# A second up-projection group planned as four tile pairs by seven products instead of three, with a different set of tiles whose low parts come by adding transfers

## The chip, the core and the metric

The kernel runs on one core of a Trainium2 chip. Its time is the device time of one execution in microseconds (us); a time given for a kernel is the median of several executions. Engines are called as in the profile: PE (matrix products), PEld (its weight loads), DVE (vector), ACT (scalar), POOL (GpSimd), SP (sync, which only issues transfers). Matrix products write PSUM banks; everything else lies in SBUF.

## What is computed

One decoder layer on 512 tokens with 1024 channels: a convolution branch and a gated linear attention branch, merged, and then a channel mixer. The change lies in the channel mixer alone:

```python
u2 = _rmsnorm(h, norm2_g[l])
z = _causal_dwconv(u2 @ w_ffn_up[l], ffn_dw_w[l], ffn_dw_b[l])
h = h + (jax.nn.silu(z[..., :FFN_DIM]) * z[..., FFN_DIM:]) @ w_ffn_down[l]
```

`w_ffn_up` has 1024 rows and 2 x 2816 columns. In tiles of 128 columns that is 22 tiles of the first half (a, 0 to 21) and 22 of the second (b, 22 to 43); channel tile i of the mixer needs a-tile i and b-tile 22 + i. The depthwise convolution has three taps in time.

## The kernel before, in words

**Products in two parts.** Every float32 operand is split into a high part (rounded by a cast on ACT) and a low part (the rest), and a product is the sum of three: low by high, high by low, high by high (`mm3`, L538 to L544). For a weight tile, `split_weight` (L415 on) writes the high part on ACT (L427 or L457). The low part is made in one of two ways for a tile of its own: DVE subtracts (L465), or, if the tile is in the set `ADDED`, ACT writes the negative of the rounded tile (L459) and a transfer on POOL's queue adds the original from memory to it (L460). For the tiles of `ADDED` in the up projection `late_low_tile` (L563) runs all products by the high part first and the eight by the low part last.

**Plain channel tiles.** Tiles i and 22 + i are each multiplied with all 512 tokens: 8 row blocks x 3 = 24 products of 512 columns a tile, 48 a channel tile.

**Channel tiles by seven products.** `two_tiles` (L1353 on) treats tile i, tile 22 + i, the two halves of the rows and the two halves of the tokens as 2 x 2 blocks, and takes seven block products instead of eight: 7 x 4 row blocks x 3 = 84 products of 256 columns. Its weight operands come in four parts: x1 (two block products, tile i itself), x3 (two, a sum of blocks of both tiles), x2 (two), x4 (one, half as wide). POOL adds the blocks: three additions of 128x512 behind the split of x1, a fourth behind that of x3 (L399). Four block products write bank x one after the other; after three of them ACT copies an interim result out of x or y (L1360), or DVE subtracts or adds it (L1363), before the next block product may go on in the same bank. The results lie in two `tmp` tiles, c1 and c2; there are six `tmp` buffers, and each channel tile's convolution takes two more (L1739 on ACT, L1742 on DVE).

**Order.** The up projection runs in four groups' worth of channel tiles: first 0 and 2 as a start, then the lists in `PLANS`, each followed by a part of the down projection (`seven`, L1513 adds its results to `hres`). A list has entries by kind; `up_plan` turns each into a sequence of steps of PE: a part of a seven-product unit, a piece of a plain tile (row blocks a to b), or a role. A role ("first" or "second" in a pair of channel tiles) is the tail of a channel tile: convolution taps, SiLU, gating (L1756), differences and sums for the down projection (L1772, L1782 to L1784) and their splits (L1761 on ACT, L1762 on DVE). Behind the last product of a unit nothing on PE waits for its role until the down projection; a unit's x1 is moved ahead of roles that stand directly before it. In the kind `both` two units share one plain tile pair: x1, x3, a1, x2, a2, x4 of the first, then the second's x1, x3, b1, x2, b2, x4. In the kinds `opens`, "" and `closes` one unit goes with one plain channel tile, and a piece of it stands between any two successive parts of the unit (`opens` begins with a piece, too).

**Looking ahead.** `weight` splits two operands ahead of the one in use, `refill` issues loads (on SP, L309 and L305) two ahead of that; there are four raw tiles, four for high and four for low parts. A planner puts the instructions of each engine in one fixed order, by the order of the program and by its own estimates of when each can run.

Of the kernel before, what the change touches and what calls it, by code (L numbers as in the profile page):

```python
# [28 lines left out]
FT = FF // P  # L29
# [3 lines left out]
O_PAIRS = ((0, 2), (1, 3), (4, 6), (5, 7))  # L33
GROUPS = (((0, 2), (1, 3), (4, 6), (5, 7)), ((8, 10), (9, 11), (20, 21)), ((12, 14), (13, 15), (16, 18), (17, 19)))
PLANS = (
(("plain",1,3),("both",4,6,5),("closes",7,8)),(("opens",10,9),("",11,20),("closes",21,12)),(("opens",14,13),("",15,16),("",18,17),("plain",19)),)
AHEAD = 6

MERGE = [("w_gb", 6, 7), ("w_ga", 0, 1), ("w_ga", 2, 3), ("w_ga", 4, 5), ("w_ga", 6, 7)]
# [9 lines left out]
ADDED = {("w_glu", j) for j in range(4, 2 * KT)} | {("w_qk", m) for m in range(KT)}  # L49
ADDED |= {("w_v", KT // 2 + j) for j in range(KT // 2)} | {("w_gb", m) for m in range(AHEAD)}  # L50
POOLED = {("w_qk", 0), ("w_qk", 1)}
ADDED -= POOLED
ADDED |= {("w_up", j) for j in (1, 23, 3, 25, 8, 9, 31, 20, 35, 16, 39, 19, 41)}
RATE = 5.0
ROWS = (0, 5, 5, 5, 8, 8, 8, 8)
EVERY = (6, 6, 6, 6, 4, 4, 4, 4)
# [47 lines left out]
def trunk_layer(ctx: ExitStack, tc: tile.TileContext, a: dict, out: bass.AP):  # L104
# [28 lines left out]
    def heap(dt=F32):  # L133
        return hp.tile([P, T], dt, tag="h", name=nm("h"))
# [57 lines left out]
    def up_plan(gi):  # L192

        pairs = GROUPS[gi]
        whole = range(KT)

        def parts(q):
            return [("part", q, part) for part in ("x1", "x3", "x2", "x4")]

        def cut(m, *at):  # L200
            return [("tile", m, range(a, b)) for a, b in zip((0, *at), (*at, KT))]

        def turns(m, role):
            return [("tile", m, whole), ("tile", FT + m, whole), (role, m)]

        def one(q, f, kind):

            x1, x3, x2, x4 = parts(q)
            if kind == "opens":
                (a1, a2), (b1, b2, b3) = cut(f, 4), cut(FT + f, 4, 6)  # L210
                seq = [a1, x1, a2, x3, b1, x2, b2, x4, role(q), b3]
            elif kind == "closes":
                a1, a2, a3 = cut(f, 3, 6)
                seq = [x1, a1, x3, a2, x2, a3, x4, role(q), ("tile", FT + f, whole)]
            else:
                (a1, a2), (b1, b2) = cut(f, 5), cut(FT + f, 4)
                seq = [x1, a1, x3, a2, x2, b1, x4, role(q), b2]
            return seq + [role(f)]

        def both(p, q, f):  # L220

            x1, x3, x2, x4 = parts(p)
            y1, y3, y2, y4 = parts(q)
            (a1, a2), (b1, b2) = cut(f, 4), cut(FT + f, 4)
            return [*(x1, x3, a1, x2, a2, x4, y1, y3, role(p), b1, y2, b2, y4, role(q)), role(f)]

        seconds = {q for _, q in pairs}

        def role(i):
            return ("second" if i in seconds else "first", i)  # L230

        plan = []
        for kind, *units in PLANS[gi]:
            if kind == "plain":
                for i in units:
                    plan += turns(i, role(i)[0])
            elif kind == "both":
                plan += both(*units)
            else:
                plan += one(*units, kind)  # L240
        for n in range(1, len(plan)):
            at = n
            while plan[n][0] == "part" and plan[n][2] == "x1" and at and plan[at - 1][0] in ("first", "second"):
                plan[at - 1], plan[at] = plan[at], plan[at - 1]
                at -= 1
        return plan
# [32 lines left out]
    for gi, pairs in enumerate(GROUPS):  # L279
        if gi == 0:  # L280
            order += [("w_up", j) for i in pairs[0] for j in (i, FT + i)]
            first = len(order) + 6
        else:
            first = len(order)
        order += up_order(up_plan(gi))
        tight |= set(range(first, len(order)))
        order += [("w_down", (pairs, step, d)) for step, d in STEPS]
# [1370 lines left out]
    for p, q in O_PAIRS:  # L1658

        f1 = merged(p)  # L1660
        both = heap(F32R)
# [203 lines left out]
    banks, values, units = {}, {}, {}  # L1865
    third, found_parts = [], {}
    for gi, pairs in enumerate(GROUPS):
        acts = []
        if gi == 0:
# [8 lines left out]
            p, q = pairs[0]  # L1878
# [13 lines left out]
        else:  # L1892
            found = first_of_pair(w)
        for what, i, *rest in up_plan(gi):
            if what == "tile":
                if 0 in rest[0]:
# [130 lines left out]
```

## Time and profile before

| | |
|---|---|
| median of 3 runs | 819.51 us (819.47 to 819.72) |
| the profiled execution, its own time | 820.0 us |
| its span, first to last instruction | 818.3 us |
| PE busy | 807.3 us, 99% |
| DVE, ACT, POOL busy | 691.1 (84%), 501.8 (61%), 212.1 (26%) us |
| transfers | 120.43 MB, mean 147 GB/s |
| mean granted clock of PE | 0.997 |

A row of the timeline gives the start and the duration in us, the engine, the line, the operation, what it writes and reads, and in brackets how long the engine was idle before and what ended that. A product's shown duration is longer than the distance to the next one, since products are pipelined: the pace is read from the starts. The channel mixer takes PE from about 487 us on; the list of the second group (`PLANS[1]`) starts at 605.92 us, and its part of the down projection at about 669 us.

### The profile page before, as it was taken

How to read it: one execution, taken by the hardware profiler on the slowest of the kernel's cores; microseconds unless marked ns; L12 is line 12 of the kernel's file. 1: busy time of each engine (PE TensorE's matmuls, PEld its weight loads, DVE VectorE, ACT ScalarE, POOL GpSimd, SP SyncE). 2: the span in 40 equal slices, each digit the busy share in tenths (PEclk: the TensorE clock that was granted, in tenths of full speed). 3: DMA queues.
4: the chain of work that ended last, by engine and by line, in shares of the span. 5: the costliest groups of instructions: out<-in, count | busy, mean ns of one | idle time of the engine just before them, and what ended most of it. 6: DMA issues, size and time to landing. Idle time of an engine off the chain costs nothing.

```text
span 818.3 us, 11590 instructions
## 1 busy us (share of the span) xinstructions
PE 807.3 (99%) x4263; PEld 695.1 (85%) x4263; DVE 691.1 (84%) x1091; ACT 501.8 (61%) x763; POOL 212.1 (26%) x193
## 2 busy tenths in 40 slices
PE   9999999999999999999999999999999999999996
PEld 7888888888888899989888898898889987899885
DVE  6779999998998878486778888989956999688895
ACT  6667788677547565493534656567355664467544
POOL 2025433332203332122001113340133311532012
PEclk9999999999999999999999999999999999999998
DMA  8488858645831232422448544256655346446762
GB/s 334 147 196 178 187 161 189 147 123 135 182 105 48 80 127 78 153 105 88 170 131 209 177 121 112 78 180 181 130 159 175 129 107 163 129 129 209 203 129 103
DMA packets 38346, 120.43 MB, mean 147 GB/s; under 512 B 3897, under 2 KB 9153, under 8 KB 38289
## 3 DMA queue, kind: packets, MB, share of 16 engines
q1 hardware_dynamic: 28912, 86.39, 29.4%
q0 software_dynamic: 9360, 33.30, 22.8%
q8 instruction: 33, 0.54, 0.3%
q14 instruction: 25, 0.20, 0.1%
q10 hardware_dynamic: 16, 0.00, 0.0%
HBM read 117.58 MB, written 2.10 MB: 146 GB/s over the span
## 4 chain that ended last, share of the span: by engine, by line
PE 76%; DVE 18%; issue 2%; DMA 2%; ACT 1%; POOL 0%; POOLq 0%; SPq 0%; DVEq 0%; ACTq 0%
PE mm L542 15%; PE mm L543 15%; PE mm L544 15%; PE mm L563 7%; DVE c L911 5%; PE cv L542 3%; PE cv L543 3%; PE cv L544 3%; DVE aside L911 3%; DVE tmp L1742 2%; PE ax L543 2%; PE ax L544 2%; PE mm L765 2%; PE ax L542 2%; DVE wlo L428 2%
## 5 line engine op out<-in xcount | busy, mean ns | idle before, releaser
L542 PE MATMUL mm<-uh,wlo 128*128 128x512 f32 (+1 forms) x444 | 161.3, 363 | 0.0
L543 PE MATMUL mm<-ul,whi 128*128 128x512 f32 (+1 forms) x444 | 158.9, 358 | 0.0
L544 PE MATMUL mm<-uh,whi 128*128 128x512 f32 (+1 forms) x444 | 158.9, 358 | 0.0
L428 DVE TENSOR_TENSOR wlo<-raw,whi 128x1024 fp32r<-128x1024 f32 x86 | 105.0, 1227 | 36.7 <-ACT whi L427 35.2
L399 POOL TENSOR_TENSOR raw<-raw,raw 128x512 f32<-128x512 f32 x42 | 66.7, 1589 | 187.4 <-DVE wlo L428 116.1
L427 ACT CAST whi<-raw 128x1024 fp32r<-128x1024 f32 x86 | 82.6, 966 | 39.7 <-PE mm L544 26.8
L542 PEld LDWEIGHTS mm<-uh,wlo 128*128 128x128 f32 x444 | 83.9, 189 | 12.6 <-DVE wlo L465 0.3
L544 PEld LDWEIGHTS mm<-uh,whi 128*128 128x128 f32 x444 | 83.8, 189 | 12.4
L543 PEld LDWEIGHTS mm<-ul,whi 128*128 128x128 f32 x444 | 83.9, 189 | 12.0
L457 ACT CAST whi<-raw 128x1024 fp32r<-128x1024 f32 x78 | 81.3, 1046 | 20.7 <-PE mm L544 14.1
L459 ACT ACTIVATE wlo<-raw 128x1024 fp32r<-128x1024 f32 x41 | 43.2, 1059 | 34.2 <-PE mm L542 19.0
L427 ACT CAST whi<-kept 128x1024 fp32r<-128x1024 f32 (+1 forms) x40 | 40.3, 1009 | 33.7 <-DVE kept L375 16.9
L428 DVE TENSOR_TENSOR wlo<-kept,whi 128x1024 fp32r<-128x1024 f32 (+1 forms) x40 | 47.7, 1193 | 11.5 <-ACT whi L427 11.5
L911 DVE SCALAR_TENSOR_TENSOR c<-aside,btmp,c 128x247 f32<-128x247 f32 (+13 forms) x93 | 51.8, 562 | 0.0
L911 DVE SCALAR_TENSOR_TENSOR aside<-cv,pp,aside 128x255 f32<-128x255 f32 (+6 forms) x112 | 51.8, 462 | 0.0
L465 DVE TENSOR_TENSOR wlo<-raw,whi 128x1024 fp32r<-128x1024 f32 x35 | 45.2, 1299 | 5.6 <-ACT whi L457 5.4
L911 DVE SCALAR_TENSOR_TENSOR c<-cv,pp,c 128x247 f32<-128x247 f32 (+13 forms) x93 | 43.0, 463 | 1.4 <-ACT c L907 1.4
L1742 DVE SCALAR_TENSOR_TENSOR tmp<-mm,pp,tmp 128x511 f32<-128x511 f32 (+1 forms) x46 | 34.1, 742 | 4.3 <-ACT tmp L1739 4.1
L563 PE MATMUL mm<-ul,whi 128*128 128x512 f32 x88 | 34.4, 391 | 0.0
L563 PE MATMUL mm<-uh,whi 128*128 128x512 f32 x88 | 34.3, 390 | 0.0
L1742 DVE SCALAR_TENSOR_TENSOR tmp<-tmp,pp,tmp 128x511 f32<-128x511 f32 (+1 forms) x36 | 31.0, 878 | 1.5 <-ACT tmp L1739 1.2
L1360 ACT COPY tmp<-mm 128x256 f32<-128x256 f32 x32 | 11.8, 369 | 26.9 <-PE mm L544 25.7
(519 smaller groups left out, 2220.2 us busy)
## 6 DMA issues: line engine op xcount, KB each, us to landing
raw<-in_w_up_dram SPq DMA_DIRECT2D x44, 512.0 KB, 4.8
raw<-in_w_glu_dram SPq DMA_DIRECT2D x16, 512.0 KB, 5.3
raw<-in_w_down_dram SPq DMA_DIRECT2D x15, 512.0 KB, 5.9
wlo<-in_w_up_dram POOLq DMA_DIRECT2D x13, 512.0 KB, 6.9
wlo<-in_w_glu_dram POOLq DMA_DIRECT2D x12, 512.0 KB, 6.9
kept<-in_w_down_dram POOLq DMA_DIRECT2D x10, 512.0 KB, 5.7
raw<-in_w_v_dram SPq DMA_DIRECT2D x8, 512.0 KB, 6.7
raw<-in_w_qk_dram SPq DMA_DIRECT2D x8, 512.0 KB, 6.0
```

The source lines that it names most:

```text
L399: work = nc.gpsimd.tensor_tensor(out, x, y, ALU.add)
L427: nc.scalar.copy(hi, raw)
L428: two_low[:] = [nc.vector.tensor_tensor(lo, raw, hi.bitcast(F32), ALU.subtract)]
L457: nc.scalar.copy(hi, raw)
L459: pace[0] = nc.scalar.mul(lo, raw, -1.0)
L465: pace[0] = nc.vector.tensor_tensor(lo, raw, hi.bitcast(F32), ALU.subtract)
L542: nc.tensor.matmul(acc, ll, rh, start=first, stop=False, **kw)
L543: nc.tensor.matmul(acc, lh, rl, start=False, stop=False, **kw)
L544: nc.tensor.matmul(acc, lh, rh, start=False, stop=last, **kw)
L563: nc.tensor.matmul(acc, x[:, k * P : (k + 1) * P], acts[k][n], start=at == 0, stop=at == len(parts) - 1)
L911: nc.vector.scalar_tensor_tensor(out[:, j:], x[:, : half_t - j], w, out[:, j:], ALU.mult, ALU.add)
L1742: nc.vector.scalar_tensor_tensor(z[:, s:], acc[:, : T - s], w[j], z[:, s:], ALU.mult, ALU.add)
```

## The change

`PLANS[1]` gets two entries in place of three. Before, units by seven products are 10, 11 and 21, and 9, 20 and 12 are plain; after, units are 10, 9, 20 and 21, and 11 and 12 are plain. A new kind, `both_close`, orders 20, 21 and 12. The order of the roles stays 10, 9, 11, 20, 21, 12. `ADDED` loses 9, 31 and 20, and gains 5, 27, 30, 11, 33, 12 and 34, so 18 tiles of the up projection are in it where 13 were. Of the tiles that are plain in both kernels, 5, 27, 30, 12 and 34 change from DVE's subtraction to the adding transfer.

```diff
 PLANS = (
-(("plain",1,3),("both",4,6,5),("closes",7,8)),(("opens",10,9),("",11,20),("closes",21,12)),(("opens",14,13),("",15,16),("",18,17),("plain",19)),)
+(("plain",1,3),("both",4,6,5),("closes",7,8)),(("both",10,9,11),("both_close",20,21,12)),(("opens",14,13),("",15,16),("",18,17),("plain",19)),)
-ADDED |= {("w_up", j) for j in (1, 23, 3, 25, 8, 9, 31, 20, 35, 16, 39, 19, 41)}
+ADDED |= {("w_up", j) for j in (1, 23, 3, 25, 5, 27, 8, 30, 11, 33, 12, 34, 13, 35, 16, 39, 19, 41)}
+        def both_close(p, q, f):
+            x1, x3, x2, x4 = parts(p)
+            y1, y3, y2, y4 = parts(q)
+            a1, a2, a3, a4 = cut(f, 2, 4, 6)
+            return [x1, a1, x3, x2, x4, y1, a2, y3, role(p), a3, y2, a4, y4, role(q), ("tile", FT + f, whole), role(f)]
...
-            elif kind == "both":
-                plan += both(*units)
+            elif kind.startswith("both"):
+                plan += {"both": both, "both_close": both_close}[kind](*units)
```

## The prediction, made before the changed kernel ran

> **What bounds the kernel now.** I read the page first, then the list of who waited for whom on PE, the chain of waits, and the stretches of the channel mixer.
>
> ```profile
> span 818.3 us, 11590 instructions
> ...
> PE 807.3 (99%) x4263; PEld 695.1 (85%) x4263; DVE 691.1 (84%) x1091; ACT 501.8 (61%) x763; POOL 212.1 (26%) x193
> ```
>
> ```profile
> PE mm L542 <- DVE hres L1513: 0.6, 1, 0.6
> PE mm L542 <- ACT tmp L1360: 0.4, 1, 0.4
> ```
>
> ```profile
> 551.00:569.00 18.00, 18.00 (x109) 16.01 (x108) 18.00 (x28) 11.89 (x18) 1.80 (x3) 1.00 0.61 183
> 606.00:622.00 16.00, 16.00 (x103) 14.55 (x102) 8.40 (x9) 6.93 (x11) 6.95 (x6) 1.00 0.49 143
> 622.00:645.00 23.00, 23.00 (x151) 21.01 (x150) 19.36 (x27) 14.87 (x21) 7.47 (x6) 1.00 0.39 115
> 645.00:660.00 15.00, 15.00 (x101) 13.76 (x100) 14.17 (x20) 9.54 (x15) 1.74 (x1) 1.00 0.48 169
> ```
>
> PE is the bound: busy without a hole in all four stretches (columns: length, then busy us of PE, PEld, DVE, ACT, POOL; clock, transfer share). So time is won only by fewer columns on PE or by ending one of its short waits, and is lost wherever a new wait begins. DVE is full in two places, 551 to 569 and 645 to 660, where the roles of channel tiles pile up, so there it covers little more.
>
> **The change part by part: products.** One channel tile goes from 48 products of 512 columns to 84 of 256.
>
> ```profile
> 761.74 10.88 PE mm L563 x48
> ```
>
> ```profile
> 608.64 0.28 PE L542 MATMUL cv<-uh,wlo 128*128 128x256 f32 x1
> ...
> 611.51 0.40 PE L563 MATMUL mm<-uh,whi 128*128 128x512 f32 x1
> ```
>
> The chain holds 48 wide products in 10.88 us, 0.2267 each. Between the two starts of the timeline lie 24 narrow ones: 2.87 us, 0.1196 each, over half of a wide one. 84 take 10.05, so **0.83 us** goes, wherever the products are issued without a hole. The Trainium skill (TensorE: Matmul & The Clock Gate, Back-to-back issue gap) has N / 2.4 + 2.5 ns: 215.8 and 109.2 ns, which as an estimate would save 1.19 us; both rows here are longer, the narrow one by more, and I keep to them.
>
> **Low parts.** Tiles 5, 27, 30, 12 and 34 lose a subtraction of some 1.14 us on DVE, and get an ACT pass and a POOL issue, as do the new plain tiles.
>
> ```profile
> L459 ACT ACTIVATE wlo<-raw 128x1024 fp32r<-128x1024 f32 x41 | 43.2, 1059 | 34.2 <-PE mm L542 19.0 <-PE ax L542 10.4 <-PE cv L542 3.1
> ...
> L460 POOL DMA_DIRECT2D wlo<-in_w_up_dram x13 | 11.3, 868 | 49.6 <-ACT wlo L459 48.4 <-DMA raw<-in_w_up_dram 1.1
> ...
> wlo<-in_w_up_dram POOLq DMA_DIRECT2D x13, 512.0 KB, 6.9
> ```
>
> Five more passes (5 x 1.06 on ACT, 5 x 0.87 on POOL) and 2.5 MB beside 120 hide behind PE: ACT is busy 61%, POOL 26%. What they relieve is seen at two waits of PE in the first group:
>
> ```profile
> 512.32 1.21 DVE L465 TENSOR_TENSOR wlo<-raw,whi 128x1024 fp32r<-128x1024 f32 x1
> ...
> 516.19 0.74 DVE L1742 SCALAR_TENSOR_TENSOR tmp<-mm,pp,tmp 128x510 f32<-128x510 f32 x1
> ...
> 517.02 0.63 ACT L1750 ACTIVATE tmp<-tmp 128x512 f32<-128x512 f32 x1 [0.27 <-DVE tmp L1742]
> ...
> 517.25 0.28 PE L544 MATMUL ax<-uh,whi 128*128 128x256 f32 x1
> ...
> 517.56 0.35 ACT L1360 COPY tmp<-mm 128x256 f32<-128x256 f32 x1
> ...
> 517.96 0.38 PE L542 MATMUL mm<-xq,wlo 128*128 128x256 f32 x1 [0.43 <-ACT tmp L1360]
> ...
> 518.19 0.28 PE L543 MATMUL mm<-usq,whi 128*128 128x256 f32 x1
> ```
>
> Unit 4 goes from x1 to x3 with no piece between. Its copy out of bank x stands on ACT behind a SiLU that waits for a tap on DVE, and DVE is late by tile 5's subtraction (512.32), among others. PE starts 517.96 for a due 517.37, and loses another 0.11 in restarting: 0.70. Without the 1.14 the copy comes in time: **-0.70** (bounds -0.70 and 0, if ACT's extra pass takes its place).
>
> ```profile
> 557.72 1.23 DVE L465 TENSOR_TENSOR wlo<-raw,whi 128x1024 fp32r<-128x1024 f32 x1
> ...
> 577.34 1.22 DVE L428 TENSOR_TENSOR wlo<-raw,whi 128x1024 fp32r<-128x1024 f32 x1
> ...
> 578.15 0.39 PE L542 MATMUL ax<-whi,al 128*128 128x512 f32 x1
> 578.62 0.50 PE L543 MATMUL ax<-wlo,ah 128*128 128x512 f32 x1
> 578.95 0.40 PE L544 MATMUL ax<-whi,ah 128*128 128x512 f32 x1
> ```
>
> At 578 a low part of the down projection is late at the end of a DVE queue in which tile 30's subtraction stood; the two gaps of 0.47 and 0.33 exceed 0.227 by 0.34 in all: **-0.34** (bounds -0.34 and 0). The price of the transfer: tile 30's low part is due 16 products, 3.6 us, after the tile begins; 1.06 + 0.87 + 6.9 us of pass, issue and landing have to start some 5 us before the tile. Between +1.1 (pass right behind the present cast, 556.63 to 557.69) and 0; I take 0, because ACT has holes of 0.6 and 0.8 us just ahead of that cast.
>
> **The new order, `both_close`.** Unit 20's x3, x2 and x4 follow each other with nothing between, while DVE works off the roles of 9 and 11. The nearest rows are those of unit 7 in the first group: it, too, follows a `both`, whose two roles (6 and 5) fall on it; but pieces of tile 8 stand between its parts.
>
> ```profile
> 546.24 0.28 PE L542 MATMUL mm<-uh,wlo 128*128 128x256 f32 x1
> ...
> 549.85 1.78 DVE L1742 SCALAR_TENSOR_TENSOR tmp<-tmp,pp,tmp 128x511 f32<-128x511 f32 x1
> ...
> 553.81 0.74 DVE L1742 SCALAR_TENSOR_TENSOR tmp<-tmp,pp,tmp 128x510 f32<-128x510 f32 x1
> ...
> 554.66 0.37 ACT L1360 COPY tmp<-mm 128x256 f32<-128x256 f32 x1 [0.64 <-DVE tmp L1742]
> ...
> 559.80 0.41 DVE L1363 TENSOR_TENSOR tmp<-tmp,mm 128x256 f32<-128x256 f32 x1
> ...
> 560.36 0.29 PE L542 MATMUL mm<-uh,wlo 128*128 128x256 f32 x1
> ```
>
> Count from x1's first product, 546.24. The copy that x2 has to wait for cannot start before the role's taps free a `tmp` buffer (553.81), and ends 8.79 us on. In `both_close` x2 is due after x1, a piece of six and x3: 2.87 + 1.36 + 2.87 = 7.10. **+1.74**, with the 0.05 from copy to product seen at 517.91 (bounds 0, if the planner gives c2 a buffer earlier, and 1.74). Behind the waiting x2 stands all of PE.
>
> Then x4 has to wait for a subtraction out of the same bank. Unit 7's ended at 13.97, 0.15 us before its x4 (560.36). `both_close` wants it at 7.10 + 1.74 + 2.87 = 11.71. Bounds 0 and +2.26; I take the row's place less the 1.14 that tile 30's subtraction held in that queue: **+1.1**. What follows gets no further wait in the sum, since each of these gives DVE and POOL time.
>
> The start of the list, `both` directly behind the down projection, costs nothing: DVE is busy 8.4 of 16 us there and ACT 6.9. POOL's four more additions (1.6 us each) fit its 26%. The largest wait left stays:
>
> ```profile
> 683.16 0.87 POOL L389 DMA_DIRECT2D kept<-in_w_down_dram  x1 [0.33 <-issue]
> ...
> 692.25 0.62 ACT L427 CAST whi<-kept 128x512 fp32r<-128x512 f32 x1 [2.18 <-DMA kept<-in_w_down_dram]
> ...
> 693.35 0.39 PE L544 MATMUL mm<-whi,yh 128*128 128x512 f32 x1
> ...
> 694.34 0.47 PE L542 MATMUL mm<-whi,al 128*128 128x512 f32 x1 [0.61 <-DVE hres L1513]
> ```
>
> An adding transfer of the down projection lands 9 us after its issue, and PE loses 0.99 - 0.23 + 0.08 = 0.84. Roles 21 and 12 and the last tile end the list as before, so 0 (bounds -0.84 and 0).
>
> **Sum:** -0.83 - 0.70 - 0.34 + 1.74 + 1.1 = +0.97 us. It is made in the profiled execution (820.0 us, 1.7 outside its span), which stands 0.5 above the median; the difference is carried to the median: 819.51 + 0.97 = **820.5**.
>
> **The rivals.** *The order costs nothing.* The planner knows the list and may put copy and subtraction ahead of role work, as nothing else on PE hangs on that; both waits near 0. Then -1.87: 817.6, or 816.8 with the wait at 694 gone too; with the waits half there 819.1. For it: in the rows it lets short instructions into the holes of chains of taps. Against: in unit 7 the subtraction stood behind ten us of role work though its product was ready 2.3 us earlier.
>
> *DVE's backlog under POOL's additions* (the slower end). Unit 21's blocks can be loaded only when 20's raw tiles come free, so POOL adds them just while DVE works off roles 9 and 11.
>
> ```profile
> 606.03 1.23 DVE L428 TENSOR_TENSOR wlo<-raw,whi 128x1024 fp32r<-128x1024 f32 x1 [1.66 <-ACT whi L427]
> ...
> 617.35 2.66 POOL L399 TENSOR_TENSOR raw<-raw,raw 128x512 f32<-128x512 f32 x2 [6.03 <-DMA raw<-in_w_up_dram]
> ...
> 618.77 2.31 DVE L428 TENSOR_TENSOR wlo<-raw,whi 128x1024 fp32r<-128x1024 f32 x1 [1.97 <-ACT whi L427]
> ```
>
> The same subtraction takes 1.23 alone and 2.31 beside an addition: 1.08 more. With the subtraction for x4 at unit 7's place (2.26) and one or two such delays ahead of it, the waits come to 5.1 to 6.2, the change to +3.2 to +4.3: 822.7 to 823.8. It decides from waits of 3.5 us together on. The Trainium skill (SBUF — State Buffer, Who interferes with whom) says that a vector instruction with two SBUF inputs and a GpSimd one that reads SBUF shut each other out for a whole instruction; the rows agree, and by it four more additions speak against the change.
>
> *The transfers relieve nothing.* DVE's freed time is taken by other late work or the low parts land late; the waits at 517 and 578 stay while the new ones come: -0.83 + 2.84 = +2.0, 821.5.
>
> **How the numbers follow.** About 0.2%, 1.64 us, is what a measurement of this kernel can tell from no change. Forecast 0.40, inside that bound, own range 818.2 to 821.1. Order free 0.26, of which 0.14 is faster by more and 0.12 lies within. Backlog 0.27 and transfers 0.07, both slower by more. So faster 0.14, same 0.52, slower 0.34. The range runs from the free order, 817.4, to the backlog's 823.6.
>
> **What would show it.** Right: no wait at x3 of unit 4 and none at 578's place; PE waiting for L1360 at x2 of unit 20 and for L1363 at its x4; 84 products of 256 columns at 0.12 for unit 9 and unit 20. Wrong: a list of 62 us without a hole on PE (order free), x4 of unit 20 or x1 or x3 of 21 waiting over 3 us, low parts of 30, 33 or 34 as PE's releaser, or a new wait in the third group, whose list is unchanged but planned anew.

## The result, and the profile after

The changed kernel takes 826.24 us (median of 4, 824.67 to 827.43) beside 819.49 for the kernel before (819.04 to 819.72): **+6.75 us, ratio 1.0082 (95% interval 1.0064 to 1.0100)**. The forecast was 820.5, with a range from 817.4 to 823.6. Its profiled execution took 826.04 us. In the ratios below, disturbed executions are left out; this matters for two of the experiments, and one profile could not be used for that reason.

One correction to the text above: the list of tiles in the change leaves out tile 13 (plain, third group), which also gets an adding transfer; with it the 18 are complete. Its cost is tried below.

All lines of the changed file stand 7 further down: L542 is L549, L563 is L570, L1360 is L1367, L1363 is L1370, L428 is L435, L1742 is L1749, L399 is L406; in the experiments some lines stand a few further down again, by their own edits. The page, and the list of who waited for whom on PE (us in total, times, longest):

```profile
span 824.3 us, 11690 instructions
...
PE 809.6 (98%) x4299; PEld 697.8 (85%) x4299; DVE 692.7 (84%) x1091; ACT 509.1 (62%) x774; POOL 221.6 (27%) x202
```

```profile
PE cv L549 <- DVE wlo L435: 2.8, 1, 2.8
PE mm L549 <- ACT tmp L1367: 2.2, 2, 1.5
```

The two waits of before (0.6 behind `hres`, 0.4 at x3 of unit 4) are gone from the list, and longer ones are there. By stage, from the starts on PE:

| stretch | before | after | change |
|---|---|---|---|
| start of the second group's list | 605.92 | 605.70 | -0.22 |
| that list | 63.04 | 69.44 | +6.40 |
| its down projection | 29.58 | 30.30 | +0.72 |
| third group's list | 73.92 | 73.92 | 0 |

So 6.9 us are lost up to the last product; what follows it happens to be 0.9 shorter in this execution (spans 818.3 and 824.3). Nearly all of it lies in the changed list. Rows of the timeline: x3 of unit 4, x4 of unit 7, tile 30 and the down projection in the first group, then the parts of units 20 and 21 in the changed list, and one wait of its down projection:

```profile
517.02 0.39 PE L549 MATMUL mm<-xq,wlo 128*128 128x256 f32 x1
...
559.82 0.39 PE L549 MATMUL mm<-uh,wlo 128*128 128x256 f32 x1 [0.23 <-DVE tmp L1370]
...
564.77 0.39 PE L570 MATMUL mm<-ul,whi 128*128 128x512 f32 x1
565.06 2.11 PE L570 MATMUL mm<-uh,wlo 128*128 128x512 f32 x8
...
578.49 0.50 PE L550 MATMUL ax<-wlo,ah 128*128 128x512 f32 x1 [0.22 <-DVE wlo L435]
...
641.82 0.39 PE L549 MATMUL mm<-xq,wlo 128*128 128x256 f32 x1 [0.63 <-ACT tmp L1367]
...
646.05 0.37 ACT L1367 COPY tmp<-mm 128x256 f32<-128x256 f32 x1 [0.65 <-DVE tmp L1749]
646.48 0.39 PE L549 MATMUL mm<-btmpq,wlo 128*128 128x256 f32 x1 [1.53 <-ACT tmp L1367]
646.59 1.06 ACT L434 CAST whi<-raw 128x1024 fp32r<-128x1024 f32 x1
...
647.37 2.73 POOL L406 TENSOR_TENSOR raw<-raw,raw 128x512 f32<-128x512 f32 x2 [4.89 <-DVE w L1763]
647.78 1.16 DVE L1779 TENSOR_TENSOR w<-w 128x256 f32<-128x256 f32 x1
648.86 1.78 DVE L1763 TENSOR_TENSOR f<-tmp,tmp 128x512 f32<-128x512 f32 x1
649.68 0.40 PE L570 MATMUL mm<-ul,whi 128*128 128x512 f32 x1
650.06 1.71 POOL L406 TENSOR_TENSOR raw<-raw 128x512 f32<-128x512 f32 x1
650.57 2.28 DVE L435 TENSOR_TENSOR wlo<-raw,whi 128x1024 fp32r<-128x1024 f32 x1
652.91 0.39 PE L549 MATMUL cv<-uh,wlo 128*128 128x256 f32 x1 [2.83 <-DVE wlo L435]
...
653.97 0.38 PE L551 MATMUL cv<-uh,whi 128*128 128x256 f32 x1
...
657.50 0.28 PE L549 MATMUL mm<-uh,wlo 128*128 128x256 f32 x1
...
689.01 0.50 PE L550 MATMUL mm<-wlo,sh 128*128 128x512 f32 x1 [0.75 <-DVE wlo L435]
```

Read the changed list from PE's three waits. What PE loses is counted from the time at which the next product was due by the pace, and the "restart" is the extra 0.1 us between the first product after a wait and the second. **x3 of unit 20** (641.82) loses 0.89 with its restart: the copy out of bank x is late on ACT. **x2 of unit 20** (646.48) loses 1.80: its copy could not start before a tap on DVE had freed a buffer. **x1 of unit 21** (652.91) loses 3.10: its low part, whose high part was ready at 647.65, ran only from 650.57 to 652.85, behind two operations of a role. POOL was adding unit 21's blocks (647.37 to 651.77) beside all three operations. They took 1.16, 1.78 and 2.28 us; the same ones take 0.41, 0.68 and 1.21 to 1.23 elsewhere (rows below), 2.9 us less. From 653.97 to 657.50 there are 17 products of 256 columns: 0.21 us each instead of 0.12, 1.5 us lost. The stretches show why:

```profile
650.00:652.90 2.90, 0.08 (x1) 0.00 (x0) 2.90 (x3) 1.56 (x2) 1.77 (x2) 1.00 0.13 51
653.90:657.40 3.50, 3.50 (x19) 3.50 (x19) 3.50 (x7) 1.18 (x2) 0.46 (x1) 0.52 0.00 0
```

Columns: length, busy us of PE, PEld, DVE, ACT, POOL, clock, transfer share, GB/s. About 1 us after PE has restarted from its hole, the granted clock is 0.52 for 3.5 us. Together 0.89 + 1.80 + 3.10 + 1.5 - 0.83 for the saved columns = 6.46, of 6.40 seen.

In the first group, whose list is unchanged, x3 of unit 4 (517.02) lost 0.70 and now loses 0.18. Tile 30's products by the low part begin 0.29 after the one before instead of 0.227. Two things take most of the gain back. x4 of unit 7 (559.82), which did not wait before, now waits for its subtraction and loses 0.43, and 0.1 in restarting. And the wait at 578, which lost 0.34 before, is still there and loses 0.50. So the second list starts only 0.22 earlier, although PE was 0.94 ahead at x3 of unit 4. In the second down projection the wait of 0.84 at 694 is gone, and one that loses 1.15 with its restart stands at 689.01.

### The profile page after: what moved, and what is told of

Its sections match the earlier page's. It is cut to its first block, busy times and chain, and to the rows that moved or that the text cites. A ratio compares the mean times of both kernels' runs of the same rounds, so it can differ in the third digit from the quotient of the medians.

```text
span 824.3 us, 11690 instructions
## 1 busy us (share of the span) xinstructions
PE 809.6 (98%) x4299; PEld 697.8 (85%) x4299; DVE 692.7 (84%) x1091; ACT 509.1 (62%) x774; POOL 221.6 (27%) x202
## 4 chain that ended last, share of the span: by engine, by line
PE 77%; DVE 17%; issue 3%; ACT 2%; DMA 1%; POOL 0%; POOLq 0%; ACTq 0%; DVEq 0%
PE mm L549 15%; PE mm L550 15%; PE mm L551 15%; PE mm L570 6%; DVE c L918 5%; PE cv L549 3%; PE cv L550 3%; PE cv L551 3%; PE cv L570 3%; DVE aside L918 3%; DVE tmp L1749 2%; PE mm L772 2%; PE ax L550 2%; PE ax L551 2%; PE ax L549 2%
## 5 line engine op out<-in xcount | busy, mean ns | idle before, releaser
L549 PE MATMUL mm<-uh,wlo 128*128 128x512 f32 (+1 forms) x412 | 146.5, 356 | 0.2 <-DVE tmp L1370 0.2
L550 PE MATMUL mm<-ul,whi 128*128 128x512 f32 (+1 forms) x412 | 144.0, 350 | 0.0
L551 PE MATMUL mm<-uh,whi 128*128 128x512 f32 (+1 forms) x412 | 144.0, 350 | 0.0
L435 DVE TENSOR_TENSOR wlo<-raw,whi 128x1024 fp32r<-128x1024 f32 x90 | 108.7, 1216 | 34.8 <-ACT whi L434 33.8
L406 POOL TENSOR_TENSOR raw<-raw,raw 128x512 f32<-128x512 f32 x45 | 68.8, 1528 | 189.6 <-DVE wlo L435 109.7
L549 PEld LDWEIGHTS mm<-uh,wlo 128*128 128x128 f32 x412 | 78.2, 190 | 11.3 <-DVE tmp L1370 0.7
L550 PEld LDWEIGHTS mm<-ul,whi 128*128 128x128 f32 x412 | 78.2, 190 | 10.4
L551 PEld LDWEIGHTS mm<-uh,whi 128*128 128x128 f32 x412 | 78.2, 190 | 10.2
L435 DVE TENSOR_TENSOR wlo<-kept,whi 128x1024 fp32r<-128x1024 f32 (+1 forms) x40 | 47.2, 1181 | 9.3 <-ACT whi L434 7.8
L570 PE MATMUL mm<-ul,whi 128*128 128x512 f32 x112 | 43.8, 391 | 0.0
L570 PE MATMUL mm<-uh,whi 128*128 128x512 f32 x112 | 43.7, 391 | 0.0
L472 DVE TENSOR_TENSOR wlo<-raw,whi 128x1024 fp32r<-128x1024 f32 x28 | 35.3, 1271 | 5.6 <-ACT whi L464 5.4
L1749 DVE SCALAR_TENSOR_TENSOR tmp<-tmp,pp,tmp 128x511 f32<-128x511 f32 (+1 forms) x40 | 35.0, 891 | 3.8 <-ACT tmp L1746 3.2
L1367 ACT COPY tmp<-mm 128x256 f32<-128x256 f32 x41 | 15.1, 369 | 31.9 <-PE mm L551 30.1
L467 POOL DMA_DIRECT2D wlo<-in_w_up_dram x18 | 15.6, 867 | 62.7 <-ACT wlo L466 50.2
```

The lines of the kernel that those rows point to most:

```text
L406: work = nc.gpsimd.tensor_tensor(out, x, y, ALU.add)
L435: two_low[:] = [nc.vector.tensor_tensor(lo, raw, hi.bitcast(F32), ALU.subtract)]
L472: pace[0] = nc.vector.tensor_tensor(lo, raw, hi.bitcast(F32), ALU.subtract)
L549: nc.tensor.matmul(acc, ll, rh, start=first, stop=False, **kw)
L550: nc.tensor.matmul(acc, lh, rl, start=False, stop=False, **kw)
L551: nc.tensor.matmul(acc, lh, rh, start=False, stop=last, **kw)
```

## The experiments

First theory: the order of the new list costs it, by DVE's queue under POOL's additions, and the hole in PE costs the clock on top. Rivals: the added transfers cost it (theory 2), or a fourth unit of seven products does, in whatever order (theory 3). Every ratio is to the kernel before on the same chip, whose medians there were 819.3 to 820.1.

**1. The order alone.** The new list with the old set:

```diff
-ADDED |= {("w_up", j) for j in (1, 23, 3, 25, 5, 27, 8, 30, 11, 33, 12, 34, 13, 35, 16, 39, 19, 41)}
+ADDED |= {("w_up", j) for j in (1, 23, 3, 25, 8, 9, 31, 20, 35, 16, 39, 19, 41)}
```

> The new list of the second group with the old set of tiles that get adding transfers, so that DVE subtracts the low parts of 5, 27, 30, 11, 33, 12 and 34 again. Theory 1 (the list's order makes the new waits: DVE's queue of the roles of 9 and 11 under POOL's additions for unit 21): at least as slow as the changed kernel, 826 to 829 us, with PE waiting at x3 and x2 of unit 20 and at x1 of unit 21 again, and with the first group's waits of 0.70 and 0.34 us back as before. Theory 2 (the added transfers with their ACT passes and POOL issues made the loss): within 1 us of the time before, 819 to 820.5. Theory 3 (a fourth unit of seven products in this group is what cannot be fed, in whatever order): as theory 1.

823.81 us, ratio 1.0054 (1.0041 to 1.0068): +3.7, between the theories. The three waits are there (0.88, 1.69 and 2.70 lost), but in the profiled execution, the fastest of the six, the half clock is not:

```profile
650.20:652.70 2.50, 0.14 (x1) 0.00 (x0) 2.50 (x2) 1.56 (x2) 1.53 (x1) 1.00 0.10 37
652.70:656.20 3.50, 3.33 (x27) 3.33 (x28) 3.50 (x9) 1.18 (x2) 0.00 (x0) 1.00 0.00 0
```

PE's list takes 67.74 us, 1.70 less than the changed kernel's: the half clock, and waits that are 0.5 shorter.

**2. The transfers alone.** The old list; 5, 27, 30, 12 and 34 join the old set.

> The list of before, with the adding transfers for 5, 27, 30, 12 and 34 beside the tiles that had them already (18 tiles). Theory 1: the transfers alone cost nothing and win what the first group showed, 0 to 1 us less than before: 818.5 to 819.7. Theory 2: most of the 6.75 us stays, 823 or more. If the gain of the first group is taken back by tile 30's late low part and by the wait at x4 of unit 7, as in the trace of the changed kernel (0.94 us won at unit 7's x1, 0.22 left at the end of the group), the time is within 0.3 of before.

822.36 us, ratio 1.0020 (1.0008 to 1.0032), and twelve executions from 819.19 to 823.46. So theory 2 holds in part: +2.3 at the median. The profiled execution (819.23, one of the two fastest) shows no wait for the landing of a transfer. In it, the landing of 30's and 34's transfers comes 0.3 and 0.9 us ahead of the first product by them, that of 5's, 27's and 12's 7.9, 2.5 and 4.0 us ahead (issue in POOL's timeline, plus landing time, against PE's timeline). That gave theory 4: only those two cost time.

**3. 5, 27 and 12 alone; 30 and 34 alone.** The old list both times.

> The list of before with adding transfers for 5, 27 and 12 beside the 13 tiles that had them; 30 and 34 keep DVE's subtraction. Theory 4 (of the added transfers only those of 30 and 34 cost time: in every trace so far theirs land 0.01 to 0.9 us ahead of their first product or just when PE already waits for them, while the others land 2 us ahead or more): the wait at x3 of unit 4 becomes shorter and nothing else changes, 0 to 0.8 us less than before, with the small spread of before (about 2.4 us on this chip). Theory 2 in its general form (ACT passes, POOL issues and traffic cost it, whichever tile): 1 to 2 us more than before.

> The list of before with adding transfers for 30 and 34 alone beside the 13 tiles that had them. Theory 4: all of the loss of the kernel with the transfers alone (2.0 us at the median), with its spread of some 4 us: 820.5 to 823.5 in the single executions, because PE waits for the landing of two transfers that come in 6 to 10 us after their issue; at a median 1.5 to 2.5 us over before. Theory 2 in its general form: two fifths of that, 0.5 to 1 us over before.

819.04 us, ratio 0.9984 (0.9975 to 0.9992), 818.04 to 819.55: **1.0 us faster than before**, with a small spread. And 821.65, ratio 1.0015 (1.0002 to 1.0029): 1.6 slower. Theory 4 holds in sign and about in size; the two do not add up to the 2.3 of the five together, so the split is rough. The kernel with 30 and 34, ACT, POOL and PE:

```profile
558.30 1.06 ACT L459 ACTIVATE wlo<-raw 128x1024 fp32r<-128x1024 f32 x1
...
559.77 0.87 POOL L460 DMA_DIRECT2D wlo<-in_w_up_dram  x1 [7.97 <-ACT wlo L459]
...
566.41 0.39 PE L563 MATMUL mm<-ul,whi 128*128 128x512 f32 x1
567.43 2.11 PE L563 MATMUL mm<-uh,wlo 128*128 128x512 f32 x8 [0.63 <-DMA wlo<-in_w_up_dram]
```

The pass for 30 stands on ACT behind the cast (557.35), the transfer lands 7.6 us after its issue, and PE loses 0.79. In four traces with the change's set this place lost 0.06, 1.12, 1.00 and 1.20, in that of 2 nothing. But the late landing is not all. In the six traces in which tile 30 has the transfer, x4 of unit 7 waits for its subtraction and loses 0.40 to 0.43; in none of the others does it. In the trace of 30 and 34 alone the second down projection takes 1.7 longer than before, with 0.89 and 0.69 lost at low parts from DVE. And no trace shows PE waiting for tile 34's transfer. So what is shown is that the pair costs time; what 34 alone costs is not. In the kernel with the other three, x3 of unit 4 starts 0.19 after the product before it, without a wait listed; it loses 0.18 with its restart, 0.52 less than before. The second list starts at 605.23, 0.69 earlier.

**4. Tile 13 as well,** which the forecast had overlooked.

> The list of before with adding transfers for 5, 27, 12 and 13. Tile 13 lies in the third group, whose list took 73.92 us in the traces of before and of the changed kernel alike, so its transfer should change nothing: within 0.5 us of the kernel with 5, 27 and 12 alone, 0.5 to 1.5 us less than before. If tile 13's transfer lands late: a wait at its last eight products in the third group.

818.99 us, ratio 0.9988 (0.9979 to 0.9997). Tile 13 costs nothing that can be told.

**5. The changed kernel without the transfers of 30 and 34.**

> The changed kernel, with tiles 30 and 34 alone back at DVE's subtraction. Theory 4 (in the transfers' share, only the two that land when they are due cost time): PE's wait in tile 30 (0.13 to 1.1 us in the traces) and the one ahead of 34's last eight products go, the waits of the new list at x3 and x2 of unit 20 and x1 of unit 21 stay: 823.3 to 825.0, as the new list with the old transfers (823.8). If all the added transfers share the cost: 825.5 or more.

823.61 us, ratio 1.0050 (1.0035 to 1.0066): as the order alone. So of the 6.75, some 2.5 come with these two transfers (with intervals of over a microsecond on both sides). Part of that may be indirect: with the two low parts on DVE the planner put x1 of 21 where it did not wait, and x3 of 21 waited 1.4 instead, in the profiled execution without the half clock.

**6. POOL writes where it added, for x1 of unit 21.**

```diff
         if part == "x1":
...
             three = raw_tile()
             pair_raws[name, p].append(three)
+            if (name, p) == ("w_up", 21):
+                for half in (three[:, left], three[:, right]):
+                    tc.keep_in_program_order(nc.gpsimd.memset(half, 0.5))
+                return
```

> The changed kernel, but POOL writes the constant 0.5 into the three blocks that belong to unit 21's x1 part, where it added (this kernel leaves out those three sums). POOL reads nothing there, and its two long blocks of additions from 647.4 to 651.8 us become short fills. Theory 1 with POOL's share: DVE's three operations of 1.16, 1.78 and 2.28 us go back to about 0.45, 0.70 and 1.23, the wait of 3.0 us at x1 of unit 21 shrinks to 0.3 to 1.0, and the stretch of half clock behind it disappears: 821.5 to 823.5 us. If DVE's queue alone makes that wait, and POOL's additions add nothing: 825.5 to 826.5.

823.66 us, ratio 1.0043 (1.0030 to 1.0055), 3.2 less than the change by the differences to before. DVE at the same operations:

```profile
648.86 0.41 DVE L1783 TENSOR_TENSOR w<-w 128x256 f32<-128x256 f32 x1
649.19 0.68 DVE L1767 TENSOR_TENSOR f<-tmp,tmp 128x512 f32<-128x512 f32 x1
649.79 1.21 DVE L439 TENSOR_TENSOR wlo<-raw,whi 128x1024 fp32r<-128x1024 f32 x1
```

0.41, 0.68 and 1.21 us, x1 of 21 goes without a wait, the clock stays 1.00, and the list takes 65.56. The waits at x3 and x2 of unit 20 stay (0.98 and 1.70). So POOL's additions beside DVE's operations are what made the third wait. That it is the reading in them, and not POOL's being busy, this run does not show: its fills ran from 643.50 to 644.48, and POOL was idle beside the three rows above. Experiment 13 has operations beside fills.

**7. Four DVE operations less ahead of x1 of 21.** In the convolution the loop over the taps is empty for `m in (11, FT + 11)`.

> The changed kernel without the four tap operations of DVE in the convolution of channel tile 11 (this kernel leaves out two of the three taps for that tile). They stand in DVE's queue between unit 20's copies and x1 of unit 21 and take 3.0 us or more. If DVE's queue sets the waits: x1 of unit 21 waits under 0.7 us where it waited 3.0, the half clock behind it does not come, and perhaps x2 of unit 20 gains too: 4.7 us less from these two, 2.5 to 5 us less in all, 821 to 824. If POOL's additions or the transfers are late by themselves: 825 or more, with the wait still over 2 us.

> The kernel without the four tap operations of channel tile 11 once more (two of the three taps of that tile are left out), for its profile. Its undisturbed runs lay at 825.5 to 829.9. If DVE's queue sets the waits, the wait of 3.0 us at x1 of unit 21 is gone or shorter in the profile, and as much or more is lost at another place that the new order of the queues made: then the time is the planner's and not these operations'. If the wait of 3.0 us is still there with three us less in DVE's queue, DVE's queue is not its cause.

Ratio 1.0098 (1.0081 to 1.0114), then 828.44 us: no gain at all. The profile of the second:

```profile
649.98 1.52 DVE L1789 TENSOR_TENSOR v<-w,f 128x256 f32<-128x256 f32 x1
651.42 1.77 DVE L1769 TENSOR_TENSOR al<-f,ah 128x512 fp32r<-128x512 f32 x1
653.11 1.48 DVE L1790 TENSOR_TENSOR v<-v,w 128x256 f32<-128x256 f32 x1
654.52 1.21 DVE L435 TENSOR_TENSOR wlo<-raw,whi 128x1024 fp32r<-128x1024 f32 x1
```

The planner moved the next operations of the role up. Beside the additions they took 4.77 us instead of 1.51, each some 1.1 longer, and the wait was 3.3. By these rows, what counts is how many operations stand ahead of the low part while POOL adds, rather than how long they are. My expectation failed because the order is planned anew.

**8. A filled hole.** 13 products of 128 columns, results unused, behind unit 20's x2:

```diff
+        if (name, p) == ("w_up", 20):
+            for _ in range(13):
+                nc.tensor.matmul(z[:, :P], ones, ones, start=True, stop=True)
```

> The changed kernel with 13 more products of 128 columns (of a constant, into a bank that is free at that place, results unused) behind unit 20's x2, in the hole of 3 us that PE has ahead of x1 of unit 21. The waits stay, since nothing else moves. Theory 1 with the clock's share: the granted clock stays at 1.00 behind the hole, where it was 0.52 from 653.9 to 657.4 us, and 1.2 to 1.7 us come back: 824.3 to 825.2, with a smaller spread between executions than the 2.8 us of the changed kernel. If the half clock is no consequence of the hole: 826 to 827.5, with a stretch of half clock at the same place.

827.93 us, ratio 1.0095 (1.0079 to 1.0110): not what I expected, and no clean test, since the planner moved x4 of unit 20 behind the filling, where it waited 2.56 for a subtraction, with half clock 1.3 us after. Tried again in 10.

**9. Pieces between the parts of unit 20, or of both units** (30 and 34 subtracted, as in all that follow).

```diff
-            a1, a2, a3, a4 = cut(f, 2, 4, 6)
-            return [x1, a1, x3, x2, x4, y1, a2, y3, role(p), a3, y2, a4, y4, role(q), ("tile", FT + f, whole), role(f)]
+            a1, a2, a3 = cut(f, 3, 6)
+            return [x1, a1, x3, a2, x2, a3, x4, y1, y3, role(p), y2, y4, role(q), ("tile", FT + f, whole), role(f)]
```

> The changed kernel with pieces of tile 12 between x3, x2 and x4 of unit 20 (cut at three and six rows; the piece behind y1, and those behind role 20 and y2, are moved there), and with 30 and 34 subtracted by DVE. Theory 1: the waits at x3 and x2 of unit 20 (0.8 and 1.7) go or shrink below 0.3 together, and x1 of unit 21, which now comes six row blocks later, waits less than 1 us, without a stretch of half clock: 818 to 821. Theory 3 (a fourth unit of seven products cannot be fed in this group, in whatever order): the waits come at other places, 823 or more. Bound: x2, x4 and x3 of unit 21 now follow each other without a piece, and may wait in their turn.

For both units: `[x1, a1, x3, a2, x2, a3, x4, y1, b1, y3, role(p), b2, y2, b3, y4, role(q), role(f)]`.

> The changed kernel with pieces between the parts of both units (x1, a, x3, a, x2, a, x4 of unit 20; x1, b, x3, b, x2, b, x4 of unit 21), so that no whole tile is left for the end of the list, and with 30 and 34 subtracted by DVE. Theory 1: no wait over 0.5 us at any part of 20 or 21: the products' 0.83 us are won, 817.5 to 819.5, unless the last roles, which now have no tile of 5.4 us behind them, make the down projection wait (up to 2 us more). Theory 3: 823 or more.

825.11 us, ratio 1.0059 (1.0046 to 1.0073), and 1.0093 (1.0077 to 1.0109). The waits at x3 and x2 of 20 went (0.23 left), but x4 now waited for its subtraction, 3.6 and 3.7 us, and the half clock followed. The first theory, that the places of the pieces are all that matters, falls: theory 3 had said 823 or more. In the second, the down projection, with no whole tile ahead of it, lost another 3.9.

**10. That hole filled,** by 14 such products right ahead of x4.

> As the kernel with pieces between the parts of unit 20 (825.1), with 14 products of 128 columns of a constant (results unused) right ahead of x4 of unit 20, where PE waits 3.6 us for DVE; 26 such instructions took 3.06 us, so these 28 take 3.3 and leave a hole of some 0.3. Nothing else moves. If the hole makes the half clock (0.66 in the five us from 655 on): the granted clock stays 1.00, and 1.3 to 1.8 us come back, 823.2 to 823.9. If the half clock has another cause: 825 to 825.6, with the same slow stretch.

827.90 us, ratio 1.0104 (1.0089 to 1.0119). The clock:

```profile
655.60:660.20 4.60, 4.55 (x39) 4.35 (x37) 3.23 (x3) 3.51 (x4) 3.43 (x3) 1.00 0.00 0
660.20:664.60 4.40, 0.00 (x0) 0.00 (x0) 2.83 (x4) 1.69 (x5) 0.36 (x1) 0.75 0.49 179
664.70:668.10 3.40, 3.40 (x16) 3.40 (x17) 1.90 (x3) 1.32 (x3) 0.00 (x0) 0.50 0.52 160
```

Behind the filled hole PE runs x4 and the next part at 1.00, where the run of 9 had 0.58; behind the hole that follows it falls to 0.50. So this half clock comes from the hole. That no time came back was not only the next wait: the filling also held a weight cast of unit 21 back by 5 us (it waited for PE), and x3 of unit 9, far ahead of the filling, lost 1.38 that the run of 9 had not lost, so "nothing else moves" was wrong, and what the half clock costs is not measured by this run; the 1.5 us come from the starts in the changed kernel.

**11. Roles apart.** First, as 9, with role 11 behind x1 of 21:

> As the kernel with pieces between the parts of unit 20 (825.1), but the role of 11 is moved from the end of the first list entry to behind x1 of unit 21, so that only unit 9's role is on DVE while unit 20 runs. Theory 5 (the kind `both` keeps unit 9's role back until its end, where 11's stands too, so that two roles of some 9 us of DVE fall on unit 20's copies and subtractions): the wait of 3.6 us at x4 of unit 20 shrinks below 1 us, the stretch of half clock goes, 818.5 to 821.5, unless the parts of 21, which have no pieces between them, now wait in their turn. Theory 3 (four units of seven products cannot be fed in this group in any order): the waits only move, 823.5 or more.

Then two orders with pieces between nearly all parts of all four units. The first:

```diff
+                (a1, a2, a3), (b1, b2, b3) = cut(f, 3, 6), cut(FT + f, 3, 6)
+                return [x1, a1, x3, a2, x2, a3, x4, y1, role(p), b1, y3, b2, y2, b3, y4, role(q)]
...
+            (a1, a2, a3), (b1, b2, b3, b4) = cut(f, 3, 6), cut(FT + f, 2, 3, 4)
+            return [x1, a1, x3, a2, x2, a3, x4, y1, role(11), b1, y3, b2, y2, role(p), b3, y4, role(q), b4, role(f)]
```

> The four units each with pieces of a plain tile between all their parts, and the roles apart: role 10 behind x1 of unit 9, role 9 behind x1 of 20, role 11 behind x1 of 21, role 20 behind x2 of 21, 21 and 12 at the end with half a plain tile between; 30 and 34 subtracted by DVE. Theory 5: no wait over 0.5 us in the list, which takes 62.2 to 63 us (63.0 before), and at most 1 us more of waits in the down projection, where three roles now come late: 817.5 to 820. Theory 3: the waits come elsewhere, in the list or in the down projection, 823 or more.

The second takes `b3` and `b4`, tile 33's last pieces, into unit 20: `[x1, b3, x3, b4, x2, a1, x4, y1, role(11), a2, y3, a3, y2, role(p), a4, y4, role(q), ("tile", FT + f, whole), role(f)]`.

> A second spread order: a plain piece between nearly all parts of 10, 9, 20 and 21, two pieces fewer in the early units and tile 33's last four pieces in unit 20, so that the whole of tile 34 (5.4 us) stands between the roles of 21 and 12 again as in the kernel before; 30 and 34 subtracted by DVE. If only the pile-up of tails costs: list of 62.2 to 63 us and a down projection within 1 us of the 29.6 before, 817.5 to 820.0. If DVE has no room for a fourth unit in this stretch: 821.5 to 824, with the waits in the list or in the down projection.

Ratios 1.0066 (1.0053 to 1.0079; 825.03 us), 1.0032 (1.0020 to 1.0044; 822.14) and 1.0040 (1.0025 to 1.0055; 822.20). In the first of the three, as expected, x4 of unit 20 loses only 0.43 and no half clock comes; but 1.84 are lost ahead of the list, 1.27 and 1.60 at x2 of unit 20 and x3 of unit 21, and 3.9 in the down projection. List and down projection of the first spread order, and two stretches of the latter:

```profile
605.69:667.91 62.22, 62.22 (x433) 58.15 (x432) 49.91 (x67) 38.31 (x58) 23.50 (x17) 1.00 0.52 139
667.91:701.82 33.91, 31.17 (x127) 24.39 (x126) 29.86 (x44) 15.97 (x22) 6.69 (x7) 0.95 0.59 134
...
677.00:685.00 8.00, 5.26 (x21) 3.26 (x20) 8.00 (x12) 2.03 (x3) 1.33 (x2) 1.00 0.37 82
685.20:688.70 3.50, 3.50 (x10) 2.69 (x9) 3.07 (x5) 1.90 (x4) 1.04 (x2) 0.52 0.86 134
```

(The first two stretches are the list and its down projection, from the starts on PE.) The list has no hole and takes 62.22 us, 0.82 less than before: the products' gain, as worked out. But the down projection takes 33.91 instead of 29.58. There the tails of roles 20, 21 and 12 fill DVE ahead of the operands that it prepares for the down projection's weights:

```profile
PE ax L553 <- DVE wlo L438: 1.2, 1, 1.2
...
PE mm L552 <- ACT whi L437: 1.0, 1, 1.0
```

The second spread order has a whole tile between the last two roles again. Its down projection takes 31.34, 2.6 less than the first's, but its list takes 63.98, with 1.65 lost at one x4 that waits for its subtraction (633.81). So the time is the same: what was won at the tails was lost elsewhere.

**12. The amount of DVE work,** on the kernel before:

```diff
-        nc.vector.tensor_tensor(out, za, zb, ALU.mult)
+        for _ in range(4 if i == 20 else 1):
+            nc.vector.tensor_tensor(out, za, zb, ALU.mult)
```

> The kernel before with the same list, the same products and the same transfers, but the gating product of channel tile 20 written four times instead of once: three more operations of 0.68 us on DVE at about 658 us, 2.0 us in all, with the same result; about what a further unit adds to DVE in this list and its down projection (77.9 us busy in the kernel before, 79.8 in the first spread order). If DVE has no room from the middle of the list to the middle of the down projection: 1 to 2.5 us over before, with PE waits in the down projection. If DVE has room there and only the order of the parts and roles matters: within 0.4 us of before.

820.51 us, ratio 1.0012 (1.0003 to 1.0021): 2.0 us more on DVE cost 0.6 at the median (0.2 to 1.7 by the interval), between the two expectations. The profiled execution, the fastest of the eleven, has a new wait in the down projection, for a low part from DVE, and lacks that at 694:

```profile
682.65 0.50 PE L543 MATMUL mm<-wlo,sh 128*128 128x512 f32 x1 [0.52 <-DVE wlo L428]
```

So the amount of work may cost something, but at most 1.7, less than the 2.2 or more of every order tried: where the work falls counts, too.

**13. The first spread order without POOL's reading:** the edit of 6 for units 10, 9, 20 and 21.

> The first spread order, with POOL writing the constant 0.5 into two blocks instead of adding three, for each of the units 10, 9, 20 and 21 of the second group (this kernel leaves out those twelve sums). If DVE's operations beside POOL's reading are what the fourth unit cannot afford in any order: the down projection goes back from 33.9 to 30 to 31.5 us, the list stays at 62.2, and the time is 818.0 to 820.0. If the loss is the late roles' place alone: 821.5 to 822.5, with the same waits in the down projection.

822.15 us, ratio 1.0032 (1.0020 to 1.0044), the same as with the additions. Its list and down projection, and PE's waits there:

```profile
606.40:668.62 62.22, 62.22 (x433) 58.17 (x432) 46.62 (x67) 38.26 (x58) 11.60 (x14) 1.00 0.50 139
668.62:700.94 32.32, 29.60 (x128) 23.25 (x126) 29.79 (x44) 16.05 (x22) 6.69 (x7) 1.00 0.61 138
```

```profile
PE ax L557 <- DVE wlo L442: 1.2, 1, 1.2
...
PE mm L556 <- ACT whi L441: 1.0, 1, 1.0
```

The same waits stay (a third, of 0.5, too), with POOL busy 11.60 us in the list instead of 23.50. So in this spread order it is not POOL; what is left is the late place of the tails. The down projection is 1.6 shorter than with the additions, since the half clock did not come this time.

This run also has what 6 lacks, DVE's operations beside a fill:

```profile
627.76 0.75 DVE L1756 SCALAR_TENSOR_TENSOR tmp<-tmp,pp,tmp 128x510 f32<-128x510 f32 x1
627.90 0.99 POOL L420 MEMSET raw<- 128x512 f32 x2 [4.17 <-DVE wlo L442]
628.61 0.69 DVE L1770 TENSOR_TENSOR f<-tmp,tmp 128x512 f32<-128x512 f32 x1
```

The first lies inside the fill but for its start, the second begins inside it; they take 0.75 and 0.69, as with POOL idle. In the changed kernel operations of the same two lines took 1.76 and 1.78 beside additions (the second is shown above):

```profile
640.23 2.25 POOL L406 TENSOR_TENSOR raw<-raw,raw 128x512 f32<-128x512 f32 x1 [3.32 <-DVE wlo L435]
641.26 1.76 DVE L1749 SCALAR_TENSOR_TENSOR tmp<-tmp,pp,tmp 128x511 f32<-128x511 f32 x1
```

Of the experiments, the versions that beat both kernels are those of 3 and 4: the old list with transfers for 5, 27 and 12, with or without 13.

## Why the prediction was wrong, point by point

- **PE is the bound:** right before and after (98% busy); all of the loss is waits and clock on PE.
- **Products, -0.83:** right. The list without waits measured -0.82. That the formula was short for the narrow product "by more" holds only in proportion: 10.4 ns there, 10.9 for the wide one.
- **Tile 5's subtraction, -0.70:** right in kind. -0.52 at x3 of unit 4, in the change as in the kernel with 5, 27 and 12.
- **Tile 30: -0.34, and 0 for the transfer.** Wrong. The wait at 578 went in five of the six traces with this transfer, but not in that of the change. For the transfer I had bounds of 0 and +1.1 and took 0, since ACT had holes ahead of the cast. The pass came behind the cast, and 0 to 1.20 us were lost at the low part in the six traces. The wait at x4 of unit 7 (0.40 to 0.43, and the restart) I did not see: with tile 30's subtraction gone, its own subtraction was put behind one more operation of the role (559.35 in the change). I gave 34's transfer, lost among "the new plain tiles", no price of its own; it lands shortly ahead (0.9 in the trace of 2), and PE does not wait for it in any trace. The two together cost some 2.5 of the 6.75.
- **x2 of unit 20, +1.74 by the copy behind the taps:** right in mechanism; 1.69 to 1.70, and 0.11 for the restart, in the change and in the runs with its order of unit 20. That the size fits is in part luck: the copy ended 9.66 us after x1's first product (636.76), not 8.79, but x2 was due later, too, by what x3 had lost.
- **x3 of unit 20:** 0.89 that was not in the sum; its copy stood behind two activations of the roles on ACT.
- **x4 of unit 20, +1.1:** not in the change, since the planner ran two products of tile 12 and most of x1 of unit 21 first; it came, with 3.6, when pieces stood between the parts.
- **"What follows gets no further wait in the sum, since each of these gives DVE and POOL time."** This is the step that failed. DVE did not use the time of PE's waits for what PE needed next: its queue held the role's operations ahead of the low part, and POOL's additions fell on them. That cost 3.10 us at x1 of unit 21, and 1.5 of half clock behind it, for which the prediction had no term.
- **The rivals:** "DVE's backlog under POOL's additions" had the mechanism, the row (1.23 against 2.31) and the sign at which to look, x1 of 21 waiting over 3 us. It was priced with "one or two such delays", 3.2 to 4.3; there were three, worth 2.9 by themselves, and the clock. The Trainium skill (SBUF — State Buffer, Who interferes with whom) says that a vector instruction with two SBUF inputs contends with a GpSimd one that reads SBUF, not with one that only writes it. The runs agree: 1.78 beside additions and 0.69 beside fills. (The prediction's "for a whole instruction" goes beyond this rule.) "The transfers relieve nothing" was half right: they relieve unit 4, but two of them land with under 1 us to spare, and tile 30's brings the wait at x4 of unit 7.
- **The kept transfer's wait, 0:** it left 694, but 1.15 came at 689.01, and the down projection is 0.72 longer.
- **The sizes together:** 6.9 us were lost up to the last product where 0.97 were forecast. Of the 5.9 between, 4.6 lie at and behind x1 of unit 21, 0.9 at x3 of unit 20, 0.8 in the first group's missing gain and 0.7 in the down projection; the 1.1 at x4 did not come.

Shown: the third wait is due to POOL's additions beside DVE's operations; in the change the half clock follows the hole, and goes with it; the pair 30 and 34 bears the transfers' loss; in the first spread order the loss is in the down projection, and not due to the additions. That the late tails cause it is argued from the waits, not tested alone. Not settled: how much of the 2.5 with 30 and 34 is late landing and how much the planner's other order; whether an order exists in which the fourth unit pays. Each of the five others tried lost 2.2 us or more.

## What to carry to other kernels

Where PE is full and another engine nearly so, price a reordering by the last operand that each part waits for, and follow it past the first wait: time that PE loses is not time that the queue gains. Count the operations of DVE ahead of that operand while POOL reads, rather than their length. Before giving a low part to a transfer, subtract pass, issue and landing from the time when it is due; here the transfers with 2.5 us or more to spare paid, and with the pair that had under 1 us the gain turned into a loss that changed from execution to execution.

## What the runs showed of the hardware

- Holes of 2.56 to 4.50 us in PE (idle time, six traces) were followed by 2.9 to 3.5 us at half clock (granted 0.50 to 0.59 in the stretches); in the change this lost 1.5 us. A hole of 2.53 us was not, in the trace of the order alone; so close to 2.56, length alone need not be what decides. The half clock came 0 to 1.3 us after the restart. In the first spread order 3.5 us at 0.52 followed three short waits of 1.2, 1.0 and 0.5 us, and without POOL's reading the same three were followed by none. The Trainium skill (TensorE: Matmul & The Clock Gate, Part 1) has a free-running window of 3.4 us whose idleness halves the clock. The length of the slow stretch agrees, but holes shorter than such a window were enough here (2.56 and 2.83 us).
- Beside POOL's additions each DVE operation with two inputs from SBUF took 0.75 to 1.1 us more, a short one (0.41 to 1.16 or 1.52) much as a long one (1.21 to 2.28). Beside POOL's fills it took no more (0.75 and 0.69).
- An adding transfer of 512 KB landed 5 to 11 us after its issue, and the same one in the same place 6.9 to 8.0 in four traces.
